# Even and odd heads' products on 64 rows in every batch of two recurrences

## The chip, the core and the metric

One core of one Trainium2 chip runs the whole program. The metric is the device time of one execution in microseconds (us). Engines are called as in the profile: PE is TensorE (PEld its weight loads), DVE VectorE, ACT ScalarE, POOL GpSimd, SP SyncE.

## The reference

A backbone of two layers works on 512 latent tokens and 256 context tokens of 1024 channels. Each layer has a mixer (an RWKV-7 branch in both directions and a Hyena branch, merged by gates) and a mixture of experts. The change lies in the RWKV branch, a generalized delta rule over 8 heads of 64 channels:

```
def step(state, inp):                       # state (B, H, 64 v, 64 k)
    r_t, w_t, k_t, v_t, ka_t, kb_t = inp    # ka = -kk, kb = kk*a
    sa = einsum('bhvk,bhk->bhv', state, ka_t)
    state = state * w_t[:, :, None, :] + sa[..., None] * kb_t[:, :, None, :] + v_t[..., None] * k_t[:, :, None, :]
    y = einsum('bhvk,bhk->bhv', state, r_t) if emit else None
```

It runs over the context, then over the latent tokens from the context's final state, forwards and backwards. In the last layer the context's outputs y are not needed.

## The kernel before

The recurrence is computed in chunks of 64 tokens. `Rwkv.run` (from line 549) goes through six batches n = 0 to 5; a batch holds 128 tokens (two chunks c) of each direction d. For each batch and direction:

- `front` (line 232) makes the decayed operands: T (queries and keys times the running decay P) and K2 (keys over the decay). Heads lie in pairs j = 0 to 3 on the partitions: the even head of a pair on partitions 0 to 63, the odd one on 64 to 127. K2 has an index h of its own for even and odd, and `front` writes K2 of h = 0 on partitions 0 to 63 alone and of h = 1 on 64 to 127 alone. For batch 0 its elementwise work is on VectorE, later on GpSimd.
- `back` (line 295) multiplies K2 with T on TensorE, one product `pE` for the even head and one `pO` for the odd head of each pair (lines 310 and 311; 314 and 315 where no outputs are wanted, in layer 1's two context batches). For each c and each two pairs jp it takes one accumulator of a PSUM bank for `pE` and one for `pO` from a ring of three. Each product is 128 columns of K2 by 192 (or 128) of T; in fp32 it shows as two records in the profile. ScalarE (lines 323 to 326) and VectorE (lines 329 to 340) then copy or mask the accumulators to U and back into T: the half of T's partitions that `front` leaves alone is written here.
- `inverse` (line 342) inverts the chunks' triangular matrices with small products of 32 rows and columns and a sequence of VectorE operations; it runs once per batch for both directions.
- `chain` (line 475) carries the state R over the batch's chunks with products of 128 rows and 64 columns (pA, pB).

The rings of T, P and U have two buffers (`RING = 2`), K2 has two as well. In batches 0 and 1 the products take 64 rows: `pE` the partitions 0 to 63 of K2 and T, `pO` the partitions 64 to 127. From batch 2 on they take all 128 rows, and the rows of K2 that don't belong to the head hold zeros. `early` (line 535) writes those zeros once per layer, with four memsets on GpSimd (lines 546 and 547).

Beside the recurrence TensorE has two other kinds of work there: `psl` (line 248, 64 rows, part of `front`) and the gate products `gp` (line 1129, 128 rows and 128 columns, 256 or 512 wide), which depend on nothing in the recurrence. All is written under a framework that puts the instructions of each engine in an order of its own by priority and expected times, and sets the semaphores from the tiles that are read and written; so the order in TensorE's queue is not the order of the lines.

Of the kernel before, what the change touches and what calls it, by code (L numbers as in the profile page):

```python
# [182 lines left out]
class Rwkv:  # L183
# [111 lines left out]
    def back(self, B, d, i):  # L295

        nc, C, pl = self.nc, self.C, self.pools
        emit = self.emit_ctx or B['pr'][d] >= 2
        U, T, K2 = B['U'], B['T'][d], B['K2'][d]

        kE, kO = (slice(0, 64), slice(64, 128)) if i < self.RING else (slice(0, 128), slice(0, 128))
        for c in range(2):
            for jp in range(2):
                pE = pl['psm'].tile([128, 2, 256], F32, name="pE", tag="psm")
                pO = pl['psm'].tile([128, 2, 256], F32, name="pO", tag="psm")
                for jj in range(2):
                    j = 2*jp + jj
                    lE = K2[kE, c, j, 0]; lO = K2[kO, c, j, 1]
                    if emit:
                        nc.tensor.matmul(pE[:, jj, 0:192], lE, T[c][kE, j, 0, :], start=True, stop=True)  # L310
                        nc.tensor.matmul(pO[:, jj, 0:192], lO, T[c][kO, j, 1, :], start=True, stop=True)  # L311
                    else:
                        v3 = lambda ap: ap.rearrange("p (b t) -> p b t", t=64)[:, ::2, :]
                        nc.tensor.matmul(v3(pE[:, jj, 0:192]), lE, v3(T[c][kE, j, 0, :]), start=True, stop=True)
                        nc.tensor.matmul(v3(pO[:, jj, 0:192]), lO, v3(T[c][kO, j, 1, :]), start=True, stop=True)
                js = slice(2*jp, 2*jp+2)
                M = C['maskR'][:, d]
                b4 = lambda ap: ap.rearrange("p j (b t) -> p j b t", t=64)
                pE4 = pE.rearrange("p j (b t) -> p j b t", t=64); pO4 = pO.rearrange("p j (b t) -> p j b t", t=64)
                Ud = U[:, d, c]  # L320
                T4 = T[c].rearrange("p j h (b t) -> p j h b t", t=64)

                nc.scalar.copy(Ud[0:64, js, 0:64], pE[0:64, :, 0:64])
                nc.scalar.copy(T[c][64:128, js, 0, 0:64], pE[64:128, :, 0:64])
                nc.scalar.copy(Ud[64:128, js, 64:128], pO[64:128, :, 128:192])
                nc.scalar.copy(T[c][0:64, js, 1, 128:192], pO[0:64, :, 128:192])
                if emit:
                    me = M[:, 1:3].rearrange("p b t -> p (b t)")[:, None, :]; mo = M[:, 0:2].rearrange("p b t -> p (b t)")[:, None, :]
                    nc.vector.tensor_tensor(Ud[0:64, js, 64:192], pE[0:64, :, 64:192], me[0:64].to_broadcast([64, 2, 128]), ALU.mult)
                    nc.vector.tensor_tensor(T[c][64:128, js, 0, 64:192], pE[64:128, :, 64:192], me[64:128].to_broadcast([64, 2, 128]), ALU.mult)  # L330
                    nc.vector.tensor_tensor(T[c][0:64, js, 1, 0:128], pO[0:64, :, 0:128], mo[0:64].to_broadcast([64, 2, 128]), ALU.mult)
                    m1 = M[:, None, 1, :]; m0 = M[:, None, 0, :]
                    nc.vector.tensor_tensor(Ud[64:128, js, 0:64], pO[64:128, :, 64:128], m1[64:128].to_broadcast([64, 2, 64]), ALU.mult)
                    nc.vector.tensor_tensor(Ud[64:128, js, 128:192], pO[64:128, :, 0:64], m0[64:128].to_broadcast([64, 2, 64]), ALU.mult)
                else:
                    m0 = M[:, None, 0, :]
                    lo, hi = slice(0, 64), slice(64, 128)
                    for (dst, src, ps_) in ((Ud[0:64, js, 128:192], pE[0:64, :, 128:192], lo), (T[c][64:128, js, 0, 128:192], pE[64:128, :, 128:192], hi),
                                            (T[c][0:64, js, 1, 0:64], pO[0:64, :, 0:64], lo), (Ud[64:128, js, 128:192], pO[64:128, :, 0:64], hi)):
                        nc.vector.tensor_tensor(dst, src, m0[ps_].to_broadcast([64, 2, 64]), ALU.mult)  # L340
# [194 lines left out]
    def early(self):  # L535
        pool, ms = self.pools['hi'], self.nc.gpsimd.memset
        self.PT, self.TT = {}, {}
        self.ring(pool, 0)
        self.K2 = [pool.tile([128, 2, 4, 2, 2, 64], F32, name=f"K2{i}", tag=f"K2{i}") for i in range(2)]
        self.nk2 = 0  # L540
        self.B = [self.new(n) for n in range(6)]
        for d in range(2):
            self.fill(d, 0)
            self.front(self.B[0], d, 0)
            t = self.K2[d]
            ms(t[64:128, :, :, 0].rearrange("p c j q x -> p (c j) (q x)"), 0.0)
            ms(t[0:64, :, :, 1].rearrange("p c j q x -> p (c j) (q x)"), 0.0)

    def run(self):
        self.setup()  # L550
# [29 lines left out]
class Kern:  # L580
# [990 lines left out]
    def moe(self, l, st):  # L1571
# [279 lines left out]
        for g, turn in enumerate(groups):  # L1851
            todo = [] if g else [ahead]
            for r in turn if g else ():
                evs = [nc.sync.value_load(eid[0:1, q:q + 1], min_val=0, max_val=15) for q in r]
                todo.append(self.expert(l, P, evs, units[r], xs.pop(r)))
            for c in range(0 if g else AHEAD[l], 6):
                late = first and g >= len(groups) - LATE[l]
                if c == 3 and g + 1 < len(groups):
                    for r in groups[g + 1]:
                        xg[r] = self.gather(l, P, units[r])  # L1860
                if c == 5 and g + 1 < len(groups):
                    for r in groups[g + 1]:
                        xs[r] = self.operands(l, P, units[r], xg.pop(r))
                for e in todo:
                    next(e)
                if late and c == 0 and g + LATE[l] == len(groups):
                    early(P)
# [311 lines left out]
```

## Time and profile before

| | |
|---|---|
| time, median of 3 runs | 3255.27 us (3248.33 to 3256.88) |
| profiled execution, own time | 3266.0 us |
| its span | 3264.0 us |
| PE busy | 2947.1 us (90%) |
| DVE busy | 1689.8 us (52%) |
| ACT busy | 1116.9 us (34%) |
| POOL busy | 574.1 us (18%) |
| mean granted TensorE clock | 0.933 |

Times in a trace count from the span's start. The granted clock is a share of TensorE's full speed: 1.00 is 2.4 GHz, 0.50 is 1.2 GHz, and a stretch's mean lies between them where both occur in it. A matmul's record runs from its start to its modelled end, so records that follow one another overlap; how fast TensorE goes is seen in the distance between starts. In a timeline, records of one line that follow each other stand as one entry with their count.

### The profile page before, as it was taken

Reading aid. Unit: us, or ns where it says so; the run is one execution under the profiler, and the core shown is the slowest. Engines: PE = TensorE matmul, PEld = TensorE weight load, DVE = VectorE, ACT = ScalarE, POOL = GpSimd, SP = SyncE. Lnnn points to the kernel's source line nnn. Section 1 sums busy time; section 2 is a strip of 40 time slices with the busy share of each in tenths; the row PEclk is TensorE's granted clock in tenths of the full one; section 3 lists DMA queues with packets and bytes.
Section 4 is the critical chain, followed back from the end, with each engine's and each line's share of the span. In section 5 each row is a group of like instructions: output and inputs, shape, how many; then the busy total and the mean of one; then the engine's idle time right before and its main releaser. Section 6 shows DMA issues by size and latency. Waiting matters only on the chain. (4 is left out here: it accounts for less than half of the span.)

```text
span 3264.0 us, 61452 instructions
## 1 busy us (share of the span) xinstructions
PE 2947.1 (90%) x25238; PEld 2019.3 (62%) x25238; DVE 1689.8 (52%) x3009; ACT 1116.9 (34%) x2275; POOL 574.1 (18%) x458
## 2 busy tenths in 40 slices
PE   8999999888988799999996999989889879999994
PEld 5877866667777566566652767646666655444551
DVE  4466525887757544434547546437876571111223
ACT  3443215555422133323422444255554221111111
POOL 1001222444005100000031001254440130000003
PEclk9999998999989799999997899987998879999998
DMA  5453283111343789998894374451112549999996
GB/s 225 135 146 106 68 279 116 55 45 49 112 158 129 277 340 358 363 348 320 330 365 164 107 224 131 148 187 57 50 50 75 198 178 355 378 397 421 380 376 248
DMA packets 220709, 689.56 MB, mean 211 GB/s; under 512 B 71781, under 2 KB 99718, under 8 KB 168968
## 3 DMA queue, kind: packets, MB, share of 16 engines
q1 hardware_dynamic: 186120, 588.36, 49.2%
q10 hardware_dynamic: 26448, 70.73, 6.1%
q0 software_dynamic: 7856, 26.49, 2.3%
q8 instruction: 202, 3.31, 0.4%
q14 instruction: 83, 0.68, 0.1%
HBM read 621.33 MB, written 64.17 MB: 210 GB/s over the span
## 5 line engine op out<-in xcount | busy, mean ns | idle before, releaser
L1967 PE MATMUL acc<-raw,x 128*64 128x256 f32 (+1 forms) x7168 | 569.6, 334 | 14.1 <-DMA raw<-in_w_exp 13.5
L1967 PEld LDWEIGHTS acc<-raw,x 128*64 128x64 f32 (+1 forms) x7168 | 358.1, 125 | 214.5 <-issue 88.4
L589 DVE TENSOR_TENSOR lo<-raw,hi 128x1024 fp32r<-128x1024 f32 x190 | 230.1, 1234 | 287.4 <-ACT hi L588 280.1
L1970 PE MATMUL acc<-raw,a 128*64 128x512 f32 (+2 forms) x1376 | 293.6, 602 | 8.0 <-DMA raw<-in_w_exp 8.0
L588 ACT CAST hi<-raw 128x1024 fp32r<-128x1024 f32 x190 | 193.4, 1048 | 258.2 <-PE px L853 116.7
L1998 DVE TENSOR_TENSOR act<-acc,act 128x256 f32<-128x256 f32 (+1 forms) x98 | 42.0, 429 | 442.8 <-PE acc L1967 400.6
L849 PE MATMUL pl<-xh,hi 128*128 128x512 f32 x560 | 228.6, 408 | 0.1
L854 PE MATMUL pl<-xh,lo 128*128 128x512 f32 x560 | 225.5, 403 | 0.5 <-DVE lo L589 0.5
L850 PE MATMUL pl<-xl,hi 128*128 128x512 f32 x560 | 224.7, 401 | 0.0
L1970 PEld LDWEIGHTS acc<-raw,a 128*64 128x64 f32 (+2 forms) x1376 | 79.1, 130 | 180.4 <-issue 159.8
L1129 PE MATMUL gp<-gx,raw 128*128 128x512 f32 (+1 forms) x352 | 176.4, 620 | 1.2 <-ACT gs L1131 1.1
L1891 POOL DMA_INDIRECT xg<-hd,idx x31 | 31.6, 1019 | 781.3 <-PE pt L1909 707.6
L849 PEld LDWEIGHTS pl<-xh,hi 128*128 128x128 f32 x560 | 107.2, 191 | 39.2 <-issue 15.7
L1993 ACT ACTIVATE act<-acc 128x256 f32<-128x256 f32 (+1 forms) x98 | 38.1, 388 | 240.6 <-PE acc L1967 201.7
L854 PEld LDWEIGHTS pl<-xh,lo 128*128 128x128 f32 x560 | 107.6, 192 | 19.6 <-issue 10.9
L2016 ACT COPY a<-pt 128x256 f32<-128x256 f32 (+2 forms) x86 | 28.6, 349 | 263.3 <-PE pt L2011 263.3
L2022 DVE TENSOR_TENSOR sum<-acc,sum 64x512 f32<-64x512 f32 x82 | 56.3, 687 | 118.7 <-ACT sum L2021 118.0
L850 PEld LDWEIGHTS pl<-xl,hi 128*128 128x128 f32 x560 | 107.5, 192 | 15.9 <-issue 8.2
L311 PE MATMUL pO<-T,K 128*128 128x192 f32 (+1 forms) x320 | 86.5, 384 | 28.5 <-DVE T L330 25.6
L852 PE MATMUL px<-xh,hi 128*128 128x256 f32 x376 | 110.7, 295 | 0.0
L856 PE MATMUL px<-xh,lo 128*128 128x256 f32 x376 | 109.8, 293 | 0.0
L853 PE MATMUL px<-xl,hi 128*128 128x256 f32 x376 | 108.9, 290 | 0.4 <-DVE xl L589 0.3
(605 smaller groups left out, 6126.2 us busy)
## 6 DMA issues: line engine op xcount, KB each, us to landing
raw<-in_w_exp SPq DMA_DIRECT2D x384, 1024.0 KB
mraw<-in_w_mod SPq DMA_DIRECT2D x64, 512.0 KB
raw<-in_w_in SPq DMA_DIRECT2D x36, 512.0 KB
rkk<-rkk SPq DMA_DIRECT2D x24, 768.0 KB
raw<-in_w_in ACTq DMA_DIRECT2D x34, 512.0 KB
mraw<-in_w_mod SPq DMA_DIRECT2D x12, 1024.0 KB
raw<-in_w_in SPq DMA_DIRECT2D x32, 256.0 KB
wb<-in_w_branch SPq DMA_DIRECT2D x32, 256.0 KB
```

The costliest lines, as they stand in the source:

```text
L311: nc.tensor.matmul(pO[:, jj, 0:192], lO, T[c][kO, j, 1, :], start=True, stop=True)
L588: self.nc.scalar.copy(hi, src)
L589: (engine or self.nc.vector).tensor_tensor(lo, src, f32(hi), ALU.subtract)
L849: mm(pl, hi[:, k], xh[:, k, L], start=f, stop=False)
L850: mm(pl, hi[:, k], xl[:, k, L], start=False, stop=False)
L852: mm(px, hi[:, k], xh[:, k, X], start=f, stop=False)
L853: mm(px, hi[:, k], xl[:, k, X], start=False, stop=False)
L854: mm(pl, lo[:, k], xh[:, k, L], start=False, stop=e)
L856: mm(px, lo[:, k], xh[:, k, X], start=False, stop=e)
L1129: nc.tensor.matmul(p[:, :n], raw[k // 4][:, k % 4], self.gx[:, k, a - T0:a - T0 + n], start=k == 0, stop=k == 7)
L1967: mm(a[w * g:w * g + w, 0:4 * w], x, raw[:, 4 * w * g:4 * w * g + 4 * w], start=k == 0, stop=k == 7)
L1970: mm(a[w * g:w * g + w], x, raw, start=k < G, stop=k >= 8 - G)
```

## The change

```diff
@@ -298,7 +298,7 @@
         emit = self.emit_ctx or B['pr'][d] >= 2
         U, T, K2 = B['U'], B['T'][d], B['K2'][d]
 
-        kE, kO = (slice(0, 64), slice(64, 128)) if i < self.RING else (slice(0, 128), slice(0, 128))
+        kE, kO = slice(0, 64), slice(64, 128)
         for c in range(2):
             for jp in range(2):
                 pE = pl['psm'].tile([128, 2, 256], F32, name="pE", tag="psm")
@@ -542,9 +542,6 @@
         for d in range(2):
             self.fill(d, 0)
             self.front(self.B[0], d, 0)
-            t = self.K2[d]
-            ms(t[64:128, :, :, 0].rearrange("p c j q x -> p (c j) (q x)"), 0.0)
-            ms(t[0:64, :, :, 1].rearrange("p c j q x -> p (c j) (q x)"), 0.0)
 
     def run(self):
         self.setup()
```

All batches now take 64 rows for `pE` and the other 64 for `pO`, and the memsets of zeros go. What is computed stays the same.

## Rows read from the trace of the kernel before

**Rows 1.** Stretches of both recurrences: from:to, length, busy us (count) by engine, PEclk, DMA.
```profile
525.00:640.00 115.00, 99.58 (x1293) 74.64 (x1292) 92.73 (x183) 74.90 (x200) 42.31 (x37) 0.87 0.19 61
640.00:845.00 205.00, 183.84 (x2924) 143.76 (x2923) 166.51 (x342) 115.89 (x339) 82.50 (x69) 0.93 0.16 48
2160.00:2262.00 102.00, 88.40 (x941) 58.23 (x941) 70.45 (x148) 64.01 (x175) 42.05 (x46) 0.82 0.26 83
2262.00:2480.00 218.00, 195.62 (x3076) 150.70 (x3070) 171.29 (x342) 120.84 (x354) 86.62 (x72) 0.90 0.17 51
```

**Rows 2.** Groups by form, 128-row products: count | busy us, mean ns | idle before.
```profile
L310 PE MATMUL pE<-T,K 128*128 128x192 f32 x256 | 69.3, 382 | 12.4 <-DVE U L334 12.3
L311 PE MATMUL pO<-T,K 128*128 128x192 f32 x256 | 68.4, 376 | 23.4 <-DVE T L330 21.5 <-ACT U L448 1.3
```

**Rows 3.** Timeline of PE, 128 rows, full clock: start, us, operation, records.
```profile
703.76 0.81 PE L311 MATMUL pO<-T,K 128*128 128x192 f32 x4
704.41 1.02 PE L1129 MATMUL gp<-gx,raw 128*128 128x512 f32 x2
```

**Rows 4.** Timeline of PE, 64 rows side by side, full clock.
```profile
594.16 0.43 PE L310 MATMUL pE<-T,K 64*128 64x192 f32 x1
594.18 0.43 PE L311 MATMUL pO<-T,K 64*128 64x192 f32 x1
...
594.75 0.32 PE L310 MATMUL pE<-T,K 64*128 64x192 f32 x1
...
595.02 0.70 PE L1129 MATMUL gp<-gx,raw 128*128 128x256 f32 x2
```

**Rows 5.** Timeline of PE, a gate product behind 64 rows, full clock.
```profile
608.38 1.13 PE L1129 MATMUL gp<-gx,raw 128*128 128x512 f32 x2
```

**Rows 6.** Timeline of PE, psl behind 128 rows, full clock.
```profile
675.29 0.49 PE L311 MATMUL pO<-T,K 128*128 128x192 f32 x2
675.71 1.04 PE L248 MATMUL psl<-la,a 64*128 64x128 f32 x7
```

**Rows 7.** Chain of waits by line: whole run, then 2262 to 2312 us.
```profile
by line: PE acc L1967 8.7%; issue 4.3%; PE acc L1970 3.9%; DMA raw<-in_w_exp 3.0%; PE gp L1129 0.7%; PE pE L310 0.5%; PE psl L248 0.5%; PE pO L311 0.4%; PE pt L2011 0.4%; DVE D L368 0.4%; PE pz L425 0.3%; PE pw L417 0.3%; PE po L593 0.3%; P
by line: PE pE L310 12.3%; PE psl L248 9.7%; PE pO L311 9.0%; PE pB L515 7.8%; issue 6.7%; PE pz L425 6.7%; PE pw L417 4.7%; DVE S L361 3.8%; PE pA L494 3.8%; DVE D L368 3.4%; PE pA L507 3.1%; ACT PB L497 3.0%; PE pw L435 2.5%; PE pB L503 2
```

**Rows 8.** Stretches of one clock: from:to, length, PE busy (count), PEclk, DMA, GB/s.
```profile
2218.50:2239.00 20.50, 18.66 (x303) 0.50 0.08 29
648.40:682.60 34.20, 32.24 (x402) 1.00 0.17 47
2276.60:2312.60 36.00, 34.81 (x533) 1.00 0.23 64
2392.60:2423.30 30.70, 30.27 (x373) 1.00 0.17 47
```

**Rows 9.** Timeline of PE at half clock, just before the clock rises.
```profile
2236.59 3.18 PE L1129 MATMUL gp<-gx,raw 128*128 128x512 f32 x4
647.22 1.49 PE L310 MATMUL pE<-T,K 128*128 128x192 f32 x4
2274.42 1.49 PE L310 MATMUL pE<-T,K 128*128 128x192 f32 x4
2327.27 1.65 PE L310 MATMUL pE<-T,K 128*128 128x192 f32 x4
```

**Rows 10.** Timeline of PE, first adjacent groups after three rises.
```profile
658.06 0.59 PE L310 MATMUL pE<-T,K 128*128 128x192 f32 x2
2289.14 0.59 PE L310 MATMUL pE<-T,K 128*128 128x192 f32 x2
2400.22 0.59 PE L310 MATMUL pE<-T,K 128*128 128x192 f32 x2
```

**Rows 11.** Timeline of DVE and PE at layer 1's first product.
```profile
2170.71 0.68 DVE L292 TENSOR_TENSOR K<-kkiP,ta 64x512 f32<-64x512 f32 x1
2171.49 0.55 PE L314 MATMUL pE<-T,K 64*128 64x128 f32 x1 [2.77 <-POOL K L547]
```

## The prediction

> **What bounds the kernel now.** I read the page's slices first, then the stretches of the two recurrences by engine, the groups of the changed lines, the timeline of TensorE around them, and last the chain of waits and the clock. The edit touches batches 2 to 5 of each layer's recurrence, 640 to 845 us (layer 0) and 2262 to 2480 us (layer 1). There PE is the busiest engine, 183.8 of 205 us and 195.6 of 218 us, with DVE next at 166.5 and 171.3 [rows 1]. PE's busy time counts each product's drain over the next one's start, so it flatters; the chain of waits is the better witness. Over the whole run it puts 0.5% and 0.4% of 3264 us, together 29.4 us, on L310 and L311, and all of that lies in layer 1, since the chain is only followed from 2092 us. In its stretch from 2262 to 2312 us the two lines are 21.3% of the chain, and the PE lines that the row shows add up to about 62% [rows 7]. So the products that change are on the path, but over half of that path is other TensorE work that they share the engine, and its clock, with.
>
> **What the edit removes, part 1: the rows of zeros.** L310 and L311 have 256 records each with 128 rows [rows 2]; a product is two records, so 32 groups (c, jp) per layer with 4 E and 4 O records each. With 128 rows a record starts 0.1625 us after the last: four O records from 703.76 to 704.41 us [rows 3]. With 64 rows one record alone is no faster; what changes is that E (partitions 0 to 63) and O (64 to 127) can run side by side. Batches 0 and 1 already do this and show it: E starts at 594.16, O at 594.18 us, the last E at 594.75 and the next product at 595.02 [rows 4]: eight records in 0.86 us, where eight in a row take 1.30.
>
> How often? Only where E and O stand next to each other in PE's queue. I went through all stretches of E/O records that no other product interrupts and took the smaller of the two counts: 58 records in layer 0 and 74 in layer 1, of 128 each. At 0.1625 us (0.32 at the half clock) that is 10.1 + 14.5 = 24.6 us of PE time. The other half stands apart, as four E, then chain products, then four O, because each group waits for an accumulator (three in the ring); those save nothing. Bounds: 0 (nothing overlaps) and half of all E/O time of these batches, (46.6 + 49.8)/2 = 48.2 us. I take 24.6, the present order.
>
> The Trainium skill, "TensorEngine Tiling (Array Packing)", section "Theoretical Speedup", gives up to twice the speed for a contraction of at most 64 rows. [rows 4] reach 1.5 with the borders, and only where E and O are neighbours; by the page's factor everywhere the saving would be the upper bound, and the sum below 3255 instead of 3269.
>
> **Part 2: borders.** With 128 rows the change to a gate product costs nothing: 0.65 us for four O, then two gate records in 1.02 us [rows 3]. With 64 rows it costs: the gate product starts 0.27 instead of 0.16 us behind the last E [rows 4], and two 512-wide ones take 1.13 us [rows 5] instead of 1.02, about 0.2 us a border. The reverse holds for the 64-row products of `psl`: behind a 128-row O, `psl` starts 0.42 us after a two-record group that needs 0.325, and its first record is longer too, again 0.2 us together [rows 6]. That border goes. I count 48 borders to 128x128 products and 36 to `psl` in batches 2 to 5; the chain's and inverse's products have a border either way. (48 - 36) x 0.2 = +2.4 us; bounds -7.2 (only those that go) and +9.6 (only those added).
>
> **PE time to path.** 24.6 - 2.4 = 22.2 us less PE time. A layer-1 recurrence has 256 E/O records of batches 2 to 5, 204 at 0.1625 and 52 at 0.32 us, 49.8 us, of which the chain holds 29.4: 59%. I take 59% of the saving as the path's: -13.1 us. What is late next is the evacuation (ACT and DVE copies), which is why I don't take all of it.
>
> **Part 3: the memsets.** Eight on POOL go. The row of L314 says that it sat idle 2.77 us for POOL's L547, but the K2 rows that it reads are finished by VectorE's L292 at 2170.71 + 0.68 = 2171.39 us, and it starts at 2171.49 [rows 11]: the wait changes its name and keeps its length. In layer 0 VectorE writes its part of K2 after them too. 0 us, bounds 0 and -0.1. POOL's next instruction waits for ACT anyway.
>
> **Part 4: the clock, which the edit doesn't mention.** The batches that use 64 rows already run at a mean granted clock of 0.87 and 0.82, the later ones at 0.93 and 0.90 [rows 1]: 26% and 36% of the time at 1.2 GHz against 14% and 20%. I looked at what PE did before each rise. In batches 0 and 1 five of six rises came behind gate products on the whole array, as 2236.59 us before the rise at 2239 [rows 9]; E/O work at 64 rows with small inverse products left it low for 20.5 us [rows 8]. In batches 2 to 5 three rises came behind nothing but 128-row E/O and chain products, where there is no gate product: E at 647.22 before 648.4, E at 2274.42 before 2276.6, and the like before 2392.6 [rows 9]. I expect these three to come later once E and O hold half the array each and stand apart. What follows each is 34.2, 36.0 and 30.7 us at the full clock, PE busy 32.2 of 34.2 [rows 8]. Bounds: 0 if nothing changes; if the clock stays low to the end, 100.9 us in which PE work takes twice as long, at a PE share of the chain of 62%: +62.6. I take the point where E/O groups stand side by side again between chain products, 658.06, 2289.14 and 2400.22 [rows 10]: 9.7 + 12.7 + 7.6 = 30.0 us x 0.62 = +18.6. Four more rises come behind alternating E/O and gate products (E at 2327.27 is in one); I give each one further group of gate products, 3.18 us [rows 9]: 4 x 3.18 x 0.62 = +7.9, bounds 0 and twice that.
>
> **Sum.** -13.1 + 0 + 18.6 + 7.9 = +13.4 us on the profiled execution's 3266.0 us: 3279.4. That execution was 10.7 us above the median of the runs, 3255.3; against that, 3268.7. Forecast: 3269 us, a little slower.
>
> **Rivals.**
> (a) The clock keeps its course; pairing alone counts. 3255.3 - 13.1 = 3242 us. For it: PE is as occupied as before in the phases without gate products, and where E and O run side by side the whole array works. Against it: the lower clock of the early batches, though these also have less chain work, so that the comparison is not clean. The Trainium skill, "TensorE: Matmul & The Clock Gate", Part 1, says that the gate follows how busy PE has been; by busy time alone this rival would hold.
> (b) No difference: E and O rarely meet, or pairing and clock cancel. Borders alone give 2.4 x 0.59 = +1.4: 3257 us. For it: half of the groups stand apart today, and the waits for accumulators that separate them stay.
> (c) The clock stays low through all of the three stretches: -13.1 + 62.6 + 7.9 = +57: 3313 us. Against it: the chain's products in long runs keep PE busy and the early batches did rise once behind paired E/O work.
> So (a) is the one on the other side; it decides as soon as the rises at 648, 2277 and 2393 us stay where they are.
>
> **How the numbers follow.** Forecast (3259 to 3290) 0.40, (a) (3232 to 3250) 0.24, (b) (3247 to 3263) 0.29, (c) 0.07. About 0.3%, 9.8 us, is what a measurement of this kernel can tell from no change: 3245.5 and 3265.0 are the limits. Faster: most of (a) and a little of (b), 0.23. Same: the rest of (a), most of (b), the low end of the forecast, 0.30. Slower: 0.47. A range of 3236 to 3300 leaves out the best of (a) and (c).
>
> **What would show it.** Right: L310/L311 of batches 2 to 5 with 64 rows, E and O starts some 13 ns apart where both are ready; gate products behind them with a gap of 0.27 us; mean granted clock below 0.90 in both recurrences, with longer low stretches behind 645, 2263 and 2386 us; PE's records at the same durations. Wrong: the same rises as before (then (a)), or E and O starting one after the other though adjacent (then (b)). A different order of PE's queue would move all three counts (pairs, borders, rises), and with them the forecast either way.

## The result, and the profile after

The changed kernel takes 3301.71 us (median; 3299.29 to 3310.74) where the kernel before takes 3255.76 (3248.33 to 3256.88): a ratio of 1.0151 with an interval of 1.0127 to 1.0175. That is 46 us slower. The forecast was 3269: the direction was right, the size was not, and the time lies just outside the range.

Where is the time? The queue order of the four compute engines and of SyncE is the same in both kernels, but for the eight memsets that GpSimd no longer has. So nothing moved; the same instructions run at other durations. I cut each profile at the first `psl` product and the last chain product of a recurrence. Before, layer 0 and layer 1 (columns: stretch, length, then busy time and count of PE, PEld, DVE, ACT, POOL, then the granted clock, DMA share, GB/s):

```profile
520.97:882.94 361.97, 320.29 (x4822) 246.97 (x4822) 288.27 (x588) 213.58 (x588) 125.88 (x106) 0.91 0.20 62
2159.66:2527.81 368.15, 327.90 (x4718) 238.99 (x4718) 265.47 (x541) 204.55 (x569) 128.97 (x119) 0.87 0.22 67
```

The same two recurrences after, which is also what became of the clocks of [rows 1]:

```profile
511.28:904.24 392.96, 354.37 (x4822) 266.47 (x4822) 287.49 (x588) 213.44 (x588) 121.83 (x102) 0.79 0.18 57
2176.84:2560.99 384.15, 347.08 (x4718) 249.15 (x4718) 266.19 (x541) 204.71 (x569) 124.69 (x115) 0.78 0.21 64
```

They are 31.0 and 16.0 us longer, 47.0 together, about the whole loss. (The profiled spans differ by 33.4 only: the profiled execution of the kernel before was itself 10 us above its median and that of the kernel after 2 us below, and outside the recurrences the profile after is 13.6 us shorter.) DVE and ACT are busy for the same time to 1 us, DMA is less busy, and PE alone is busier, by 53 us, though its pairs now overlap. The granted clock fell from 0.91 and 0.87 to 0.79 and 0.78. At two levels, twice the distance from 1.00 is the share of time at 1.2 GHz, so that time went from 161 us (2 x 0.09 x 362 + 2 x 0.13 x 368) to 334 us, +173. (The low stretches themselves add up to 164 and 335 us.) I call this the low time from here on.

The groups of the changed lines after, all batches, all on 64 rows:

```profile
L311 PE MATMUL pO<-T,K 64*128 64x192 f32 x320 | 102.3, 452 | 23.1 <-DVE T L330 22.1 <-ACT gs L1128 0.9
L310 PE MATMUL pE<-T,K 64*128 64x192 f32 x320 | 102.0, 451 | 11.8 <-DVE U L334 11.6
```

The mean record went from 382 and 376 ns in batches 2 to 5 [rows 2] to 451 and 452 over all batches, with the waits for evacuated accumulators unchanged. (A part of that is pairing: beside another a record is longer too, 0.43 us in [rows 4].) Two matched stages of layer 0 show it best, from the fourth inverse's first product to the fifth's and from there to the sixth's. Before, then after:

```profile
736.10:808.80 72.70, 63.74 (x944) 50.44 (x940) 58.10 (x109) 46.82 (x139) 39.13 (x32) 0.93 0.16 49
808.80:842.00 33.20, 32.18 (x672) 24.50 (x674) 26.80 (x65) 13.29 (x38) 0.00 (x0) 1.00 0.09 25
```
```profile
737.20:822.30 85.10, 75.09 (x944) 56.09 (x940) 60.79 (x114) 46.84 (x139) 39.05 (x32) 0.75 0.14 43
822.30:863.00 40.70, 40.51 (x673) 30.83 (x674) 25.04 (x60) 13.40 (x38) 0.00 (x0) 0.72 0.07 18
```

The same 944 and some 672 records take 12.4 and 7.5 us longer, at clocks of 0.75 and 0.72 where they had 0.93 and 1.00. In the first of these stages the kernel before was low for one spell, 791.8 to 802.0 us. After, the clock fell there twice, and the second spell lasted 44.4 us. Two low spells before, each whole, the second one in layer 1:

```profile
791.80:802.00 10.20, 7.35 (x16) 4.70 (x16) 9.70 (x24) 1.76 (x7) 5.66 (x5) 0.50 0.00 0
2317.50:2331.20 13.70, 9.10 (x25) 6.49 (x26) 13.10 (x31) 4.14 (x14) 5.49 (x5) 0.50 0.23 78
```

The first two rows of the next list stand in their places. These are low stretches of the kernel after, each whole (the last three stand where the clock had risen at 2392.6, 2276.6 and 648.4 us before [rows 8]):

```profile
801.00:845.40 44.40, 42.02 (x474) 29.36 (x475) 27.28 (x65) 13.48 (x39) 5.43 (x5) 0.50 0.05 16
2340.40:2377.90 37.50, 35.52 (x388) 23.30 (x388) 22.51 (x50) 14.17 (x38) 11.08 (x10) 0.50 0.07 25
749.80:770.30 20.50, 20.19 (x181) 16.20 (x181) 11.40 (x25) 8.99 (x29) 10.77 (x10) 0.50 0.15 46
2408.70:2436.00 27.30, 25.61 (x304) 22.66 (x305) 15.87 (x28) 12.48 (x40) 13.65 (x12) 0.50 0.11 35
2282.40:2302.90 20.50, 20.50 (x396) 18.41 (x390) 13.58 (x25) 11.96 (x36) 13.93 (x12) 0.50 0.28 87
630.40:657.70 27.30, 27.30 (x273) 22.83 (x266) 12.46 (x28) 12.97 (x41) 13.17 (x12) 0.50 0.11 35
```

What PE did in the longest of them, 801.0 to 845.4 us (start, us, operation, records):

```profile
802.20 1.61 PE L311 MATMUL pO<-T,K 64*128 64x192 f32 x4 [5.34 <-DVE T L330]
803.74 2.07 PE L1126 MATMUL gp<-gx,raw 128*128 128x512 f32 x2
805.77 0.98 PE L310 MATMUL pE<-T,K 64*128 64x192 f32 x2
...
811.48 1.65 PE L310 MATMUL pE<-T,K 64*128 64x192 f32 x4
813.06 1.22 PE L1126 MATMUL gp<-gx,raw 128*128 128x256 f32 x2
814.21 1.65 PE L311 MATMUL pO<-T,K 64*128 64x192 f32 x4
815.78 2.07 PE L1126 MATMUL gp<-gx,raw 128*128 128x256 f32 x4
817.79 1.65 PE L310 MATMUL pE<-T,K 64*128 64x192 f32 x4
819.36 2.07 PE L1126 MATMUL gp<-gx,raw 128*128 128x256 f32 x4
821.37 1.01 PE L311 MATMUL pO<-T,K 64*128 64x192 f32 x2
822.30 3.42 PE L417 MATMUL pw<-ZT,U 32*32 32x16 f32 x128
```

Read it against the forecast: this is the alternation of E/O groups and gate products for which one more group of gate products was allowed. Here one gate group after another passes, and the clock stays at 1.2 GHz through five of them and then through the inverse. At the dots stand one more gate group and an E/O group side by side (807.93 to 808.70 us); further pairs at 825.65, 830.57 and 841.21 us pass at 1.2 GHz as well.

### The profile page after: what moved, and what is told of

The parts are those of the page before. It is cut to its first block, busy times and chain, and to the rows that moved or that the text cites. A ratio compares the mean times of both kernels' runs of the same rounds, so it can differ in the third digit from the quotient of the medians.

```text
span 3297.4 us, 61444 instructions
## 1 busy us (share of the span) xinstructions
PE 2989.4 (91%) x25238; PEld 2042.4 (62%) x25238; DVE 1687.6 (51%) x3009; ACT 1116.5 (34%) x2275; POOL 564.8 (17%) x450
## 5 line engine op out<-in xcount | busy, mean ns | idle before, releaser
L1126 PE MATMUL gp<-gx,raw 128*128 128x512 f32 (+1 forms) x352 | 193.2, 670 | 1.2 <-ACT gs L1128 1.1
L311 PE MATMUL pO<-T,K 64*128 64x192 f32 x320 | 102.3, 452 | 23.1 <-DVE T L330 22.1
L851 PEld LDWEIGHTS pl<-xh,lo 128*128 128x128 f32 x560 | 106.9, 191 | 18.6 <-issue 9.8
L310 PE MATMUL pE<-T,K 64*128 64x192 f32 x320 | 102.0, 451 | 11.8 <-DVE U L334 11.6
```

Source lines behind the costliest of these rows:

```text
L851: mm(pl, lo[:, k], xh[:, k, L], start=False, stop=e)
L1126: nc.tensor.matmul(p[:, :n], raw[k // 4][:, k % 4], self.gx[:, k, a - T0:a - T0 + n], start=k == 0, stop=k == 7)
```

## Experiments

Four theories are in the expectations. A1: lone 64-row work doesn't raise the clock, E beside O does, like work on the whole array. A2: 64-row work also lets a clock fall that is already high. A3: each 64-row product costs clock in like measure, whether it runs beside another or not. A4: a pair does the same work in half the time, and where PE waits for others anyway the other half becomes a pause; so the pair costs clock too. Theory A in some of the expectations is A1 in a coarser form. Ratios are to the kernel before on the same chip, over 3 or 5 rounds.

**Is it the memsets, or the rows?** The rows alone: 64 rows in all batches, zeros still written.

```diff
-        kE, kO = (slice(0, 64), slice(64, 128)) if i < self.RING else (slice(0, 128), slice(0, 128))
+        kE, kO = slice(0, 64), slice(64, 128)
```

> All batches on 64 rows, the eight memsets of zeros kept (they write rows that nothing reads). Theory A (the clock: 64-row products leave TensorE at 1.2 GHz longer): as the changed kernel, 3302 us within 8, and the low-clock time in both recurrences about 330 us as there, 164 before. Rival C (the loss comes from the memsets that are gone: another start of GpSimd, another phase of everything behind it): 3256 us, as before the change.

Measured: 3305.01 us, 1.014 [1.0119, 1.0162]. The memsets are worth nothing; the rows are the whole loss.

**The other way round.** 128 rows in batches 0 and 1 too, with T's other halves zeroed on GpSimd (those memsets are not printed here), and the mixed case: 64 rows everywhere in layer 0 only.

```diff
-        kE, kO = (slice(0, 64), slice(64, 128)) if i < self.RING else (slice(0, 128), slice(0, 128))
+        kE, kO = slice(0, 128), slice(0, 128)
```
```diff
+        kE, kO = (slice(0, 64), slice(64, 128)) if i < self.RING or self.emit_ctx else (slice(0, 128), slice(0, 128))
```

> The other direction: all batches, 0 and 1 too, on 128 rows with zeros in the other half; T's unwritten half is cleared by eight longer GpSimd memsets per layer. Theory A: batches 0 and 1 lose their low stretches (31 us in layer 0, 48 us in layer 1 before); 3240 to 3254 us, a mean clock above 0.933. Rival B (borders between 64-row and 128-row products and E beside O are what counts, the clock is a by-product): the pairs of batches 0 and 1 are lost and their psl borders come back, 3258 to 3266 us.

> 64 rows in all batches of layer 0 only; layer 1 as before. Theory A: layer 0's recurrence as in the changed kernel (393 us from its first psl to its last chain product, 362 before), layer 1's as before (368 us): 3280 to 3292 us. Rival B: borders are about as many in either layer, so half of the loss, 3279; the two differ in the low-clock time, under A 160 us in layer 0 and 100 us in layer 1, under B as before.

Measured: 3253.52 us, 0.9987 [0.9971, 1.0004], for 128 rows everywhere; 3287.04, 1.0082 [1.0068, 1.0096], for layer 0 alone. The recurrences with 128 rows everywhere:

```profile
518.59:880.88 362.29, 322.02 (x4823) 249.94 (x4822) 289.79 (x588) 214.60 (x588) 134.70 (x114) 0.92 0.20 63
2158.11:2515.99 357.88, 318.66 (x4718) 234.20 (x4718) 266.73 (x541) 205.41 (x569) 136.11 (x119) 0.91 0.22 69
```

In the profile layer 1 gains 10 us by giving up its pairs, with the clock at 0.91 instead of 0.87; the time as a whole can't be told from no change. With 64 rows in layer 0 alone that layer had a clock of 0.79 and 395 us, as in the changed kernel, and layer 1 0.87 and 368 us, as before: the effect stays in the layer whose rows change.

**Streams alone: what raises the clock?** A kernel that leaves the reference's computation out and runs streams of products without pauses, each behind some 14 us of idle PE. `al` is all 128 rows, `lo` and `hi` the halves, `z` data whose upper half is zeros:

```
mm(p[:, 0:n], w[rows, 0:128], src[rows, 512:512 + n], start=True, stop=True)
64 x (pe, al) | 64 x (pe, al, z) | 64 x (pe, lo) | 32 x (pe, lo)(po, hi) | 24 x (pg, al, 512)(pe, al)(pe, al) | 24 x (pg, al, 512)(pe, lo)(pe, lo)
```

> Streams of products alone, each behind some 12 us without TensorE work; the reference's computation is left out. In order: 64 products of 128 rows; 64 of 128 rows with half of them zeros; 64 of 64 rows; 32 pairs of E and O alternating; 16 x (2 E, 2 O); 24 x (a 512-wide 128-row product, two 128-row products of 192); 24 x (the same with two 64-row products). Theory A: the first two streams rise to 2.4 GHz early and alike; the 64-row one alone stays at 1.2 GHz for longer or to its end; the alternating ones rise. Distance of starts 0.32 us low, 0.16 high whatever the rows. Rival B: the clock takes the same course in every stream; only the borders of the last differ from those of the one before, by about 0.2 us each.

Measured, in the order of the list (a stream of (pe, lo)(pe, lo)(po, hi)(po, hi) took 13.0 us, like alternating ones):

```profile
20.90:44.80 23.90, 23.86 (x128) 23.56 (x128) 0.00 (x0) 0.00 (x0) 0.00 (x0) 1.00 0.00 1
58.90:82.60 23.70, 23.62 (x128) 23.32 (x128) 0.00 (x0) 0.00 (x0) 0.00 (x0) 0.89 0.00 1
96.70:138.10 41.40, 41.33 (x128) 40.82 (x128) 0.00 (x0) 0.00 (x0) 0.00 (x0) 0.50 0.00 0
152.20:164.90 12.70, 12.66 (x128) 12.37 (x128) 0.00 (x0) 0.00 (x0) 0.00 (x0) 0.84 0.01 1
206.20:245.00 38.80, 38.75 (x144) 25.96 (x144) 0.00 (x0) 0.00 (x0) 0.00 (x0) 0.94 0.00 0
259.20:345.20 86.00, 85.98 (x144) 39.32 (x144) 0.00 (x0) 0.00 (x0) 0.00 (x0) 0.50 0.00 0
```

Lone 64-row products keep the clock at 1.2 GHz for the whole 41.4 us, with PE busy throughout. Rows of zeros raise it: their stream begins at 1.2 GHz and has 0.89 over its whole length. (The first stream began at 2.4 GHz already, so its 1.00 is no rise; the mix with 128 rows, 0.94, began at 1.2 like the others.) The last row is the low spell of the kernel in small: 512-wide products on the whole array between pairs of lone 64-row ones, 86 us at half clock, where the same mix with 128 rows takes 38.8. E beside O rises and does the work of 23.9 us in 12.7.

**Streams alone: what makes it fall?** Again without the computation: streams that first raise the clock with 64 products on 128 rows and then go over to lone 64-row products, to the mix, or to pairs, and at last a mix with 2 E, 2 O from an idle PE.

> Streams alone again, the reference's computation left out. The first three begin with 64 products of 128 rows, so that the clock is high, and go on without a pause: with 96 products of 64 rows; with 32 x (a 512-wide 128-row product, two 64-row ones); with 96 pairs of E and O alternating. The fourth begins after a pause: 24 x (a 512-wide 128-row product, two E, two O). Theory A1 (it is lone 64-row work that costs the clock; E and O side by side count like 128 rows): the third stays at 2.4 GHz, the fourth rises to it. The fall of the first two is open: under A1 with loss on both sides they drop to 1.2 GHz although TensorE never pauses; under A1 with loss on the rise alone they stay high. Rival A2 (whatever mixes with 64 rows stays low): the fourth stays at 1.2 GHz to its end, as the 512-wide products with two lone E did.

```profile
44.10:75.60 31.50, 31.45 (x193) 31.16 (x192) 0.00 (x0) 0.00 (x0) 0.00 (x0) 1.00 0.00 1
112.50:173.20 60.70, 60.70 (x193) 29.22 (x192) 0.00 (x0) 0.00 (x0) 0.00 (x0) 1.00 0.00 1
210.90:242.40 31.50, 31.48 (x385) 31.18 (x384) 0.00 (x0) 0.00 (x0) 0.00 (x0) 1.00 0.01 2
256.50:304.50 48.00, 47.98 (x240) 23.25 (x240) 0.00 (x0) 0.00 (x0) 0.00 (x0) 0.96 0.00 1
```

Without pauses nothing falls: a high clock stays high on lone 64-row work for 31.5 us, and in the mix for 60.7. A2 is out in this form; what these streams lose, they lose on the rise. Lone 64-row work with pauses was not tried in a stream.

**Every E beside its O.** If only lone products hurt, make all of them neighbours: one accumulator tile of two banks for both (a ring of one; that constant is not printed here), on 64 rows, and the same tile on 128 rows from batch 2.

```diff
-                pE = pl['psm'].tile([128, 2, 256], F32, name="pE", tag="psm")
-                pO = pl['psm'].tile([128, 2, 256], F32, name="pO", tag="psm")
+                pEO = pl['psm'].tile([128, 2, 2, 256], F32, name="pEO", tag="psm")
+                pE, pO = pEO[:, 0], pEO[:, 1]
```

> All batches on 64 rows, and E and O of a group in one accumulator tile of two banks, one in the ring instead of three single ones: both wait for the same evacuation, so they stand next to each other always. Theory A1: nearly all pairs run side by side (180 of 192 O records per layer beside an E), the clock comes back: low time of both recurrences below 230 us (335 in the changed kernel), and the time is at or below that of the same tile with 128 rows; 3250 to 3280 us. Rival A2: low time above 300 us, time above 3290 us.

> The control: the same two-bank tile, but 128 rows with zeros from batch 2 on, as before the change. One accumulator pair instead of three accumulators: TensorE waits for each evacuation (about 2 us of VectorE and ScalarE copies); 3262 to 3285 us, low time of both recurrences 160 to 230 us. Under both theories.

Measured: 3444.17 us, 1.0581 [1.0546, 1.0617], and 3438.25, 1.0562 [1.0528, 1.0595]. The times that I expected of both were far off: the ring of one costs some 5.6%, with PE waiting for evacuation. Of the question they say this much: with E and O in one tile 64 rows are still not faster than 128, though 332 of 384 records of O run beside an E, and the low time is some 450 us against 370 (clocks of 0.74 and 0.77 against 0.78 and 0.81). That was the first sign against A1 as the whole story.

**psl on 128 rows as well.** On top of 128 rows everywhere, layer 1's `psl` products run on 128 rows, with zeros in the weights' other half (printed here: the lines that write the zeros).

```diff
+                if l:
+                    nc.gpsimd.memset(t[64 - 64 * d:128 - 64 * d], 0.0)
```

> All batches on 128 rows, and in layer 1 psl too (its weights with zeros in the other direction's rows; one buffer fewer for the gates' sigmoid, because the space is short). Theory A: layer 1's low time falls below the 61 us that all batches on 128 rows had; 3235 to 3253 us. Rival B: psl is 64 rows in its own place, its borders to gate products go and those to the inverse stay; 3250 to 3256, low time as there.

Measured: 3253.42 us, 0.9982 [0.9967, 0.9996]: the only interval that lies below 1, by 0.2%, but not apart from 128 rows everywhere (0.9987). Layer 1's low time, 82 us in the profile, did not fall below 61 as Theory A had it, so a gain from `psl` is not shown.

**Rows chosen product by product.** The queue order doesn't depend on the rows, so I could read from it which products of batches 2 to 5 have one of the other sort directly beside them (163 of 256), and give 64 rows to those alone; then to the other 93 alone; then the first choice on top of the fastest kernel. (`ROWS`, not printed here, has `h` for 64 rows and `f` for 128.)

```diff
+        rows = self.ROWS[0 if self.emit_ctx else 1][i].split()[2*d:2*d+2]
+        kr = lambda h, k: slice(64*h, 64*h + 64) if rows[h][k] == 'h' else slice(0, 128)
...
-                    lE = K2[kE, c, j, 0]; lO = K2[kO, c, j, 1]
+                    kE, kO = kr(0, 4*c + j), kr(1, 4*c + j)
+                    lE = K2[kE, c, j, 0]; lO = K2[kO, c, j, 1]
```

> 64 rows only for products that stand in TensorE's queue directly beside one of the other sort (163 of the 256 products of batches 2 to 5: 74 in layer 0, 89 in layer 1), 128 rows with zeros for the other 93; the zeros are written as in the kernel before, and the queue order of every engine is unchanged. Theory A1 (lone 64-row work doesn't raise the clock, E beside O does): nearly all pairs of the change are kept and all lone full-array work of the kernel before too, so low-clock time in the two recurrences stays near the 164 us of the kernel before (under 200, where the changed kernel had 335), and the pairs give 10 to 15 us: 3238 to 3250. Rival A3 (every 64-row product delays the clock in like measure, paired or not): 163/256 of the clock's loss of some 60 us, less 13 for the pairs: about 3281, low time about 275.

> The complement: 64 rows only for the 93 lone products of batches 2 to 5, 128 rows for the 163 that stand beside one of the other sort. Theory A1: nearly all of the clock's loss and nothing for pairs: 3295 to 3315, low-clock time in the recurrences 300 us or more. Rival A3: 93/256 of the clock's loss, about 3277, low time about 225.

> The choice of rows by neighbour in all six batches, over the kernel that had 128 rows in every product of all batches and in layer 1's psl products (0.9982 of before): lone products have 128 rows in batches 0 and 1 as well, psl of layer 1 too. Theory A1: low-clock time near the 116 us that 128 rows everywhere had, and the pairs' 10 to 15 us on top: 3235 to 3245, the fastest of all. Rival A3: slower than 3253, since 246 of 384 products are on 64 rows again: about 3275.

Measured: 3283.39 us, 1.0074 [1.0052, 1.0096]; 3277.57, 1.0058 [1.0038, 1.0079]; 3273.23, 1.005 [1.0027, 1.0072]. A3 had said 3281, 3277 and 3275; A1 misses all three. A3's low time for the first, 275 us, was not met (232). Their recurrences, first with the neighbours on 64 rows, then with the lone ones:

```profile
524.10:902.55 378.45, 334.82 (x4823) 251.22 (x4822) 288.14 (x588) 213.46 (x588) 124.17 (x106) 0.85 0.19 60
2178.06:2548.04 369.98, 327.11 (x4718) 233.29 (x4718) 266.39 (x541) 204.88 (x569) 129.44 (x119) 0.84 0.21 67
```
```profile
523.67:900.67 377.00, 333.62 (x4822) 255.07 (x4822) 291.31 (x588) 213.55 (x588) 123.71 (x106) 0.86 0.19 60
2173.62:2547.71 374.09, 335.24 (x4718) 243.19 (x4718) 266.16 (x541) 204.71 (x569) 128.85 (x119) 0.84 0.21 66
```

Low time is 232 and 225 us, against 161 before: +71 for the pairs, +64 for the lone products, together 0.8 of the change's +173, as the two losses, 0.74% and 0.58%, are nearly its 1.51%. These are single profiles. The granted clock of every execution gives the low time of the whole run (2 x (1 - clock) x span, medians): 422 us before on that chip, 515 with the neighbours on 64 rows and 469 with the lone products. By it the neighbours cost +93 and the lone products +47, a proportion nearer to A3's, 163 to 93. The pairs did run: records of O within 140 ns of an E number 151 in the first, 46 before, 154 after.

**Why does a pair cost clock?** Streams without pauses said that it doesn't. In the recurrences PE waits for others. A first kernel of paced streams (computation left out) was to test that:

> Streams alone again; the reference's computation is left out. Here another engine sets the pace: each group of eight 128x192 products waits for ScalarE, which reads both accumulators of a group and does 2, 3 or 4 further 512-wide copies before it frees them, so TensorE pauses in every group, as it does in the recurrences. Each pace is run with 128-row products and with E beside O on 64 rows, from 1.2 GHz; pace 3 also behind 64 full-array products at 2.4 GHz. Theory A1 (E beside O on the two halves counts as full-array work, whatever the pauses): the clock does the same for both kinds at every pace. Theory A4 (the pair does the same work in half the time, and the pause that it leaves lets the clock stay low or fall, so a 64-row product costs clock even when it is paired; this is what the three kernels with rows by neighbour bear out): 128-row groups rise to 2.4 GHz at pace 2 and at 3 or 4 as well, where the pairs stay at 1.2 GHz at pace 3 and 4; behind full-array products at pace 3 the pairs fall back and the 128-row groups stay high or fall later.

It settled nothing: the copies that were to set the pace ran ahead of their groups, and PE with 128 rows was the bound in all streams. In the next one the copies form a chain:

```
for _ in range(groups):
    t = ps.tile([128, 2, 512], F32, name="t", tag="t", bufs=2)
    for _ in range(4):
        prod(t[:, 0], lo if kind == "pair" else al)
        prod(t[:, 1], hi if kind == "pair" else al)
    nc.scalar.copy(w2[:, 0:384] ..., t[:, :, 0:192])
    for _ in range(k):
        nc.scalar.copy(w2, w2)
```

> Streams alone; the reference's computation is left out. As in the paced run before, but now ScalarE's copies form one chain, so that they can't move ahead: a group of eight 128x192 products (16 records, E and O alternating) waits until ScalarE has read both accumulators of the group before last and done 4, 6, 8 or 12 further 512-wide copies (some 3, 4.4, 5.6 and 8 us a group). Order: from an idle TensorE, paces 4, 6, 8, 12, each with 128-row products and then with E beside O on 64 rows, 14 groups each; then paces 8 and 12 behind 64 full-array products, 10 groups each, 128 rows and then pairs. A 128-row group takes some 2.75 us at 2.4 GHz and 5.5 at 1.2, a pair group half of that. Theory A4 (a pair is full-array work of half the length, and where TensorE waits for others the other half becomes pause): 128-row groups rise at paces 4, 6 and 8, pairs at pace 4 only or not at all, so that at pace 6 or 8 the pairs run at 1.2 GHz where the 128-row groups run at 2.4; behind full-array work the pairs fall at pace 8 and 12, the 128-row groups at 12 or not. Theory A1 (pairs count as the 128-row products do, whatever the pauses): both kinds at the same clock at every pace.

Measured, with 4, 6, 8 and 12 copies, each pace with 128 rows and then with pairs, and last two rows at 8 copies behind full-array work at 2.4 GHz:

```profile
20.65:63.16 42.51, 40.75 (x224) 38.08 (x224) 0.00 (x0) 35.69 (x61) 0.00 (x0) 1.00 0.00 1
85.02:124.36 39.34, 23.61 (x224) 20.08 (x224) 0.00 (x0) 34.46 (x59) 0.00 (x0) 0.94 0.00 1
147.52:204.04 56.52, 41.10 (x224) 37.72 (x224) 0.00 (x0) 49.29 (x83) 0.00 (x0) 0.97 0.00 1
229.80:283.41 53.61, 31.73 (x224) 26.59 (x224) 0.00 (x0) 48.02 (x81) 0.00 (x0) 0.69 0.00 1
310.46:381.69 71.23, 47.95 (x224) 44.25 (x224) 0.00 (x0) 62.85 (x105) 0.00 (x0) 0.87 0.00 1
411.35:479.77 68.42, 35.57 (x224) 29.70 (x224) 0.00 (x0) 62.09 (x104) 0.00 (x0) 0.62 0.00 0
510.20:612.22 102.02, 62.71 (x224) 58.25 (x224) 0.00 (x0) 91.60 (x152) 0.00 (x0) 0.72 0.00 0
647.98:745.81 97.83, 38.71 (x224) 32.83 (x224) 0.00 (x0) 90.05 (x149) 0.00 (x0) 0.60 0.00 1
798.00:854.92 56.92, 42.77 (x217) 39.98 (x215) 0.00 (x0) 42.76 (x72) 0.00 (x0) 0.88 0.00 1
898.00:950.64 52.64, 30.24 (x213) 26.17 (x211) 0.00 (x0) 40.34 (x68) 0.00 (x0) 0.73 0.00 0
```

At the second pace the same number of products, delivered to the same consumer in nearly the same time (56.5 and 53.6 us), leave the clock at 0.97 with 128 rows and at 0.69 as pairs; at the third 0.87 and 0.62; at the fourth 0.72 and 0.60. Only at the quickest do both run high (1.00, from a clock that was high at its start, and 0.94, from a low one). Behind full-array work at 2.4 GHz it is alike: 0.88 against 0.73 at the third pace, 0.78 against 0.64 at the fourth. That is A4, on the rise and on the fall, with two differences: the 128-row groups lost some of their clock at the third pace already, where it had them keep it, and at the second the pairs rose and fell again, where it had them stay low. A1 would have had equal clocks in each couple. That a pair counts just as full-array work of half the length is not shown: no stream had 128-row groups of half the products.

## Why the prediction was wrong in size

**What fell on it.** Before the result I named the step "Four more rises come behind alternating E/O and gate products (E at 2327.27 is in one); I give each one further group of gate products, 3.18 us": +7.9 us. It allowed 4 x 3.18 = 12.7 us at half clock, and failed twice over. Gate products did not raise the clock while lone half-array work stood between them: 86 us at 0.50 in the stream, and in the kernel spells of 44.4 and 37.5 us where it had 10.2 and 13.7. The kernels with chosen rows part these two. With the lone products alone on 64 rows the spell in layer 1 is 30.7 us, with the neighbours alone 10.2: there the lone work does most of it. In layer 0 the lone products alone leave it at 10.3 us: the clock rises where it did before, in the gate products behind neighbouring E and O, which still have 128 rows. With these as pairs (807.93 us) no rise came there, and none behind the lone ones that follow.

And the step counted rises only, not that the clock would fall more often: at 671.3, 749.8, 2323.4 and 2453.1 us begin low spells with none in their places before, 10.3, 20.5, 10.2 and 6.8 us, 48 together. Why it falls there is not shown; the one at 749.8 has counterparts in both kernels with chosen rows (10.3 and 17.0 us), so it doesn't need new pairs.

The premise under it, that in batches 0 and 1 five of six rises came behind gate products on the whole array, was read rightly from the rows. That gate products therefore do it, whatever surrounds them, was not in them.

**The three pure rises: right.** They were to wait for the next E/O group side by side. After, PE's last rows before the rise at 657.7 us are these. They are the group that stands at 658.06 us in [rows 10]. The rise at 2436.0 comes behind the group that had 2400.22 there (E at 2435.73), and that at 2302.9 behind alternating E and O (O at 2301.72) a little ahead of the group forecast:

```profile
657.20 0.64 PE L310 MATMUL pE<-T,K 64*128 64x192 f32 x1
657.21 0.64 PE L311 MATMUL pO<-T,K 64*128 64x192 f32 x1
657.68 0.32 PE L310 MATMUL pE<-T,K 64*128 64x192 f32 x1
657.69 0.32 PE L311 MATMUL pO<-T,K 64*128 64x192 f32 x1
```

The spells grew from 3.4, 13.7 and 6.8 us to 27.3, 20.5 and 27.3, by 51 us; in the first and the third some 14 us of that are an earlier fall, which was not forecast. In the kernel with the zeros kept the same three are 24, 20 and 31 us. (The three distances in the prediction are 9.7, 12.5 and 7.6, 29.8 us; it has 12.7 and 30.0.)

What a us of low time costs is an estimate. The kernel with 64 rows for lone products alone has hardly any new pairs (53 of the records counted above, 46 before): +21.0 us of recurrence for +64 of low time, 0.33 per us; by its executions' clocks 20.2 us for +47, 0.43. Among the 38 executions of the kernel before, on two chips, the time rises by 0.25 and 0.21 us with each us of low time. At 0.2 to 0.43 the three rises cost 10 to 22 us (predicted 18.6), and the other 120 us of low time 24 to 52 (predicted 7.9): 58 in the two mixed spells, 48 in the four new ones, the rest mainly in batches 0 and 1, whose products are unchanged. That is the miss.

**Pairs and borders: right in kind, not sized.** E and O start 10 ns apart where they are neighbours, as in [rows 4], and 108 more records of O run beside an E (132 were counted). At 0.33 the clock would cost 173 x 0.33 = 57 us, and the recurrences lost 47.0, which leaves -10 us for pairs and borders, where -13.1 was predicted; the kernel with the neighbours on 64 rows gives 71 x 0.33 - 18.3 = 5. But at 0.2 per us the clock costs 35 us, less than was lost, and at 0.43 it costs 74. So what pairs and borders gave lies somewhere between nothing and 27 us, and -13.1 is neither borne out nor refuted.

**Memsets: right**, nothing. **Order of the queues:** I named a changed order as what could move all counts; it didn't change.

**The rivals.** (a), the clock keeps its course, is refuted; the statement of the Trainium skill behind it ("TensorE: Matmul & The Clock Gate", Part 1: the gate follows how busy PE has been) doesn't hold here in the sense of the profile's busy time, since PE was busy for 41.33 of 41.40 us at 1.2 GHz in the lone 64-row stream. (c), low through all three stretches at +57, came near the measured sum for another reason: the three stretches did rise about when forecast, and the mixed ones far later.

**Shown and not shown.** Shown: the rows are the cause, the loss is in the recurrences and is the clock, lone 64-row work does not raise it, and at a pace set by another engine a pair costs clock as well. Not shown apart: how much of the pairs' +71 us comes from rises that came later and how much from added falls. The near sum of the two chosen-row kernels hides that single spells don't add up: the one in layer 0 is 44.4 us with both sorts on 64 rows, 10.3 with the lone ones, and with the neighbours three spells of 3.4, 6.9 and 17.0. That pauses act in the recurrences as in the streams rests on the streams and on the kernels with chosen rows together; no kernel took the pauses out and kept the rest.

## What to carry to other kernels

Rows of zeros were not waste here: in stretches where PE is near its bound but waits in every group, cutting the rows in half cost granted clock, paired or not, and everything beside them in PE's queue ran slower with it. Before packing two halves of the array, look at the granted clock of a stretch that already does it, and at what stands between the halves in the queue; a gain of 0.11 us a product where two run side by side (0.44 us for four in [rows 4]) is lost to a few low spells of 20 to 40 us. And test a clock effect with pauses in the stream: without them E beside O looked free.

## What the runs showed of the hardware that I had not expected

- A stream of 64-row products with PE busy 41.33 of 41.40 us never left 1.2 GHz, even with 512-wide products on the whole array between them (86.0 us); 128-row products whose upper half is zeros did leave it (0.89 over 23.7 us).
- The two directions differ: a clock that is high stays high on that same lone work for 31.5 us, and in the mix for 60.7.
- Two ways of doing the same work in nearly the same time are granted different clocks: 0.97 with 128 rows, 0.69 as pairs with a pause behind each group.
